# Output weights split in each pass, PSUM-resident convolution sums and column-wise block sums in a hybrid decoder block

## The chip, the cores and the metric

The kernel runs on one core of one Trainium2 chip. Its engines work side by side, each through its own queue in order: TensorE (PE) multiplies, VectorE (DVE), ScalarE (ACT) and GpSimd (POOL) work element by element, SyncE (SP) only issues DMA transfers, as ACT and POOL can too. Operands lie in SBUF; PE writes its products to PSUM, which DVE and ACT read and write. The metric is the device time of one execution in microseconds (us); less is better.

## The reference, cut to what matters

One decoder layer, 16 meta tokens ahead of 1024 tokens, width 1024, two mixing groups of 512 channels, feed-forward width 2816, all fp32:

```python
def mixer(xn, w_in, conv_a_w, conv_b_w, conv_b_bias, ln_b_gain, ln_b_bias, w_out):
    h = jnp.einsum("btd,de->bte", xn, w_in)
    b_gate, c_gate, h_a, glu_val, glu_gate = jnp.split(
        h, [W_A, 2 * W_A, 3 * W_A, 3 * W_A + W_B], axis=-1)
    y_a = b_gate * causal_depthwise_conv(c_gate * h_a, conv_a_w)      # 3 taps
    g = glu_val * jax.nn.sigmoid(glu_gate)
    z = causal_depthwise_conv(g, conv_b_w) + conv_b_bias              # 31 taps
    y_b = jax.nn.silu(layer_norm(z, ln_b_gain, ln_b_bias))
    y = jnp.concatenate([y_a, y_b], axis=-1)
    return jnp.einsum("bte,ed->btd", y, w_out)

h = h + rms_norm(mixer(rms_norm(h, pre_mix_norm), ...), post_mix_norm)
h = h + rms_norm(swiglu(rms_norm(h, pre_ffn_norm), w_gate, w_up, w_down), post_ffn_norm)
```

## The kernel before

Every product is made of three fp32r matmuls (`mm3`, lines 107 to 111): each operand is split into a rounded high part (an ACT copy, names in `h`) and the rest (a subtraction, names in `l`), and high x high, high x low and low x high are summed in PSUM. The order of the instructions on each engine is that of the program text.

**Input projection.** w_in comes in 20 units of 128 output channels; a unit is a letter (g, v: gate and value of the convolution group; c, h, b: the three parts of the other group) and an index 0 to 3. Units (g,0) and (v,0) run while x arrives (lines 178 to 243). Then `UNITS` (line 142) sets the order of the other 18: g1 v1 g2 v2 g3 v3, then c h b for each index. For each unit the loop at line 495 first emits the split of the next unit's weights (`split_unit`: high part on ACT, low on POOL), the load of the one after it, then `after[...]`, which takes the previous unit out of PSUM, then what `LEAD_IN` lists for that step, and last the unit's matmuls on PE. Two units have PSUM at a time, so what takes unit i out must be done when PE begins unit i+2. `AT` puts further work between the matmuls of a step.

**Output weights.** `pre_out` (line 252) loads a 128-row unit of w_out, splits it on ACT and DVE and stores both parts to DRAM (`wo`). Units 0 and 1 are emitted ahead of the end of (v,0), 2 to 5 in step 0, 6 and 7 inside `start_g`, which also spreads the inverse norms over the partitions (`spread_x`, tile pb_x) and makes the first gate.

**Convolution of 31 taps.** Times are kept as even and odd halves of 512 columns (e and o in `gpad`). Per channel block a there are three chains of DVE operations (`taps`, line 338), each sum kept in a PSUM tile: `common` (o with summed taps), then `even` (e - o) and `odd` (a shifted difference). `common` starts from z in SBUF and ends there, and the other two start from z and end there. The two differences are DVE operations on SBUF tiles (lines 352, 353). The first eight terms of `common` for blocks 1 to 3 come from `conv_head` (ACT products, POOL additions into z). `tap(n)` in `LEAD_IN` emits the next n taps. `value` (line 309) writes the gate product into the halves.

**Layer norm.** `ln_sum`, `ln_mean`, `ln_var`, `ln_spread`, `ln_apply` in steps 13 to 16; `sums` adds the four blocks in SBUF.

**Output projection.** Three passes, `group((0,1,2))`, `group((3,4,5))`, `group((6,7))`, over token tiles; a pass takes all 8 units of w_out in the order `up` or `down_`. `next_o` fetches the split units from DRAM on POOL's queue, 18 in all. `leave_psum` and `norms` finish a tile, `turn` transposes it for the next stage.

**Feed-forward.** Both products use a seven-product block scheme. T1 to T4, B11, B21, B22 are the right operands, made from the transposed tiles (`raw`); `a_side` makes the left ones from w_gate and w_up, two products ahead, where `operand` emits the ACT copy and the DVE subtraction of one matrix and then those of the other. `order` lists the products as (pair, n); product s takes its operands from step s - 2. `Pair.leave` takes them out of PSUM.

Of the kernel before, what the change touches and what calls it, by code (L numbers as in the profile page):

```python
# [15 lines left out]
P = 128  # L16
# [41 lines left out]
def hybrid_block(ctx: ExitStack, tc: tile.TileContext, xT, x, w_in, w_out, w_gate, w_up, w_down, par, g_post, g_ffn, g_out, out):  # L58
# [81 lines left out]
    wo = [dram.tile([P, 2, D], F32R, tag=f"wo{k}", name=f"wo{k}") for k in range(KD)]  # L140
# [88 lines left out]
    split_unit(UNITS[0])  # L229
    nc.vector.tensor_tensor(sa[0], sa[0], sa[1], op=ALU.add)  # L230

# [13 lines left out]
    ws_o = {}  # L245

    def load_raw_o(k):
        if k < KD:
            ws_o[k] = yap.tile([P, D], F32, tag="y", name=f"ws_o{k}")
            nc.sync.dma_start(ws_o[k], w_out[k])  # L250

    def pre_out(k):
        load_raw_o(k + 2)
        ws = ws_o.pop(k)
        h, l = (yap.tile([P, D], F32R, tag="y", name=f"{c}_o{k}") for c in ("wh", "wl"))
        nc.scalar.copy(h, ws)
        nc.vector.tensor_tensor(l, ws, h.bitcast(F32), op=ALU.subtract)
        for q, t in enumerate((h, l)):
            nc.sync.dma_start(wo[k][:, q, :].bitcast(F32), t.bitcast(F32))
# [12 lines left out]
    mm_k(pu["v", 0], split_w["v", 0], KD - 1, 0, T3, 3)  # L272
# [36 lines left out]
    def value(a):  # L309
        o4 = new_g(a).rearrange("p r (a n) -> p a n r", a=3)  # L310
        for i in range(3):
            nc.vector.tensor_tensor(o4[:, i], pu["v", a][:, i, :T3].rearrange("p (n r) -> p n r", r=2), three(sg[a])[:, i].rearrange("p (n r) -> p n r", r=2), op=ALU.mult)
# [15 lines left out]
    def conv_head(a):  # L328

        ze, zo = halves_of(a)  # L330
        o = gpad[a][1]
        nc.scalar.activation(zo, o[:, :HALF], AF.Identity, scale=wc(a, 0), bias=pr[:, O_CBB + a : O_CBB + a + 1])
        for i in range(1, HEAD[a]):
            t = ct.tile([P, HALF], F32, tag="ct", name=f"ct{a}{i}")
            nc.scalar.activation(t, o[:, i : i + HALF], AF.Copy, scale=wc(a, i))
            nc.gpsimd.tensor_tensor(zo, zo, t, op=ALU.add)

    def taps(name, src, w, first, n, init, out):
        acc = aux.tile([P, 512], F32, tag="a", name=name)
        for i in range(first, n):  # L340
            nc.vector.scalar_tensor_tensor(out if i == n - 1 else acc, src[:, i : i + HALF], w(i), init if i == first else acc, op0=ALU.mult, op1=ALU.add)  # L341
            yield

    def common(a):
        ze, zo = halves_of(a)
        yield from taps(f"ac{a}", gpad[a][1], lambda i: wc(a, i), HEAD[a], NE, zo, zo)

    def even(a):
        e, o = gpad[a]
        ze, zo = halves_of(a)  # L350
        d = ct.tile([P, (G0 + TT) // 2], F32, tag="d", name=f"d{a}")
        nc.vector.tensor_tensor(d, e, o, op=ALU.subtract)
        nc.vector.tensor_tensor(o[:, :-1], e[:, 1:], o[:, :-1], op=ALU.subtract)
        yield from taps(f"ae{a}", d, lambda i: wb(a, 2 * i), 0, NE, zo, ze)

    def odd(a):
        e, o = gpad[a]
        ze, zo = halves_of(a)
        yield from taps(f"ao{a}", o, lambda i: wb(a, 2 * i + 1), 0, NE - 1, zo, zo)
# [10 lines left out]
    def conv():  # L370
        yield from common(0)
        yield from by_turns(even(0), odd(0))
        yield from by_turns(common(1), common(2))
        yield from by_turns(even(1), odd(1))
        yield from by_turns(even(2), odd(2))
        yield from common(3)
        yield from by_turns(even(3), odd(3))

    conv_taps = conv()
# [28 lines left out]
    def after_b(a):  # L408
        yh[a], yl[a] = (yap.tile([P, SEQ], F32R, tag="y", name=f"y{c}{a}") for c in "hl")
        for q in range(2):  # L410
            s = slice(q * HALF, (q + 1) * HALF)
            nc.vector.tensor_tensor(cv[a][:, s], pu["b", a][:, q, :], cv[a][:, s], op=ALU.mult)  # L412
        nc.scalar.copy(yh[a], cv[a])
        nc.vector.tensor_tensor(yl[a], cv[a], yh[a].bitcast(F32), op=ALU.subtract)
# [8 lines left out]
    def sums(srcs, outs):  # L423
        for q in range(3):
            for hf in range(2):
                nc.vector.tensor_tensor(outs[hf], srcs(hf, 0) if q == 0 else outs[hf], srcs(hf, q + 1), op=ALU.add)

    def ln_sum():
        ln["zs"] = [ct.tile([P, HALF], F32, tag="ct", name=f"zs{hf}") for hf in range(2)]
        sums(lambda hf, a: z[a][:, hs_[hf]], ln["zs"])  # L430

    def ln_mean():
# [8 lines left out]
        sums(lambda hf, a: ln["sq"][hf, a], [ln["sq"][hf, 0] for hf in range(2)])  # L441
# [33 lines left out]
    def start_g():  # L475
# [43 lines left out]
    ps2 = pa.enter_context(tc.tile_pool(name="ps2", bufs=6, space=PSUM, reuse_waits="tile"))  # L519

    for a in range(4):
# [6 lines left out]
        nc.vector.tensor_tensor(ol, z2, oh.bitcast(F32), op=ALU.subtract)  # L528

# [69 lines left out]
    def operand(src, name, place=None):  # L599
# [6 lines left out]
        sub(t[:, 1, :], src, t[:, 0, :].bitcast(F32))  # L606
# [11 lines left out]
    class Pair:  # L618
# [19 lines left out]
        def a_side(self, n, m, place=None):  # L638
# [21 lines left out]
            return operand(s, f"{n}_{self.j}{m}", place)  # L660
# [74 lines left out]
    wu = {}  # L735

    def load_o(k):
        wu[k] = [wp.tile([P, D], F32R, tag=t, name=f"{t}_o{k}") for t in ("wh", "wl")]
        for q in range(2):
            nc.gpsimd.dma_start(wu[k][q], wo[k][:, q, :])  # L740

    todo_o = list(range(KD)) + list(range(KD - 4, -1, -1)) + list(range(3, KD))

    def next_o():
        if todo_o:
            load_o(todo_o.pop(0))

    def group(grp, ks, at):
# [8 lines left out]
        for s, k in enumerate(ks[:-2]):  # L757
# [3 lines left out]
            if s or grp[0] == 0:  # L761
                next_o()
# [16 lines left out]
    for q, t in ((0, 0), (1, 1), (0, 1), (1, 0)):  # L779
        raw[q, t] = blocks(big(f"raw{q}{t}", F32))  # L780
# [6 lines left out]
    s1, left = group((3, 4, 5), down_, {4: turns(0, 1), 5: turns(2)})  # L787
# [49 lines left out]
    s1, left = group((6, 7), up, {6: early})  # L837
# [21 lines left out]
    def t2():  # L859
        X[6] = pair("T2", (rp, rp))  # L860
        copy_hi(X[6], T2r)
        split_lo(X[6], T2r)
# [351 lines left out]
```

## Time and profile before

| | us |
|---|---|
| median of 3 runs (lowest, highest) | 1059.92 (1058.63, 1061.58) |
| the profiled execution | 1059.18 |
| its span, first to last instruction | 1057.2 |
| input projection, (v,0) ends to (b,3) ends | 35 to 279 |
| output projection and entry of the products | 279 to 387 |
| gate and up products | 387 to 828 |
| down products and the end | 828 to 1057 |

The profile records one execution. Its page gives busy time by engine, 40 slices of the span, DMA queues and the costliest groups of instructions; other views of the trace give the same by stretch of time, the waits of each engine with what ended them, and the instructions in order. L341 is line 341 of the kernel, `ae<-d,pr,z` a write of tile ae from d, pr and z, and `x4` a count.

### The profile page before, as it was taken

The page shows a single profiled execution, that of the slowest core. Times are in us where ns is not written, and L with a number is a line of the kernel's source. Part 1 is how long each engine was busy: PE and PEld are TensorE (multiplying, and loading weights), DVE is VectorE, ACT ScalarE, POOL GpSimd, SP SyncE. Part 2 cuts the span into 40 slices and gives each one's busy share as a digit, 9 for nine tenths or more (in the row PEclk, how much of TensorE's full clock was granted, in tenths as well). Part 3 has the DMA queues.
Part 4 walks back from the last instruction along what each step waited for, and adds up shares of the span by engine and source line. Part 5 has one row for each costly group of instructions (what it writes and reads, how often), then busy time and mean ns, then how long its engine had stood idle before and what let it go on. Part 6 is the DMA issues. An engine that isn't in the chain of part 4 may idle for free.

```text
span 1057.2 us, 12732 instructions
## 1 busy us (share of the span) xinstructions
PE 986.2 (93%) x4643; PEld 839.9 (79%) x4643; DVE 773.9 (73%) x1087; ACT 378.4 (36%) x616; POOL 296.3 (28%) x267
## 2 busy tenths in 40 slices
PE   9599998879999797998999999999999899999994
PEld 8499998769787675876888888888888788888773
DVE  6689999997414558789888888888878343446667
ACT  7433331233413254333443433434334233322331
POOL 0247774443112100026134223313413522212110
PEclk9799998989999999999999999999999999999998
DMA  7851111001759552034634443353324989867765
GB/s 304 301 216 41 41 42 60 20 20 61 254 163 316 183 184 74 1 122 177 219 130 149 160 170 148 130 209 117 142 100 169 384 309 376 270 183 204 268 215 209
DMA packets 64909, 180.80 MB, mean 171 GB/s; under 512 B 6864, under 2 KB 7248, under 8 KB 64848
## 3 DMA queue, kind: packets, MB, share of 16 engines
q1 hardware_dynamic: 43344, 109.40, 28.2%
q0 software_dynamic: 16272, 59.25, 17.4%
q10 hardware_dynamic: 5232, 11.35, 3.0%
q8 instruction: 36, 0.59, 0.2%
q14 instruction: 25, 0.20, 0.1%
HBM read 122.83 MB, written 57.15 MB: 170 GB/s over the span
## 4 chain that ended last, share of the span: by engine, by line
PE 60%; DVE 26%; DMA 5%; ACT 4%; issue 4%; POOL 1%; SPq 0%; DVEq 0%; ACTq 0%; POOLq 0%
PE x L109 6%; PE x L111 6%; PE x L110 6%; PE y L109 5%; PE y L110 5%; PE y L111 5%; DVE ao L341 4%; DVE ae L341 4%; PE qx L110 3%; PE qx L109 3%; PE qx L111 3%; DVE ac L341 3%; PE qy L110 2%; PE qy L111 2%; PE qy L109 2%
## 5 line engine op out<-in xcount | busy, mean ns | idle before, releaser
L592 DVE TENSOR_TENSOR op<-u,op 128x512 fp32r<-128x512 f32 x154 | 142.9, 955 | 61.6 <-ACT op L605 61.6
L605 ACT CAST op<-u 128x512 fp32r<-128x512 f32 x154 | 90.7, 618 | 163.6 <-DVE u L592 153.6
L592 DVE TENSOR_TENSOR db<-wb,db 128x512 fp32r<-128x512 f32 x77 | 53.7, 701 | 93.2 <-ACT db L1015 92.9
L1015 ACT CAST db<-wb 128x512 fp32r<-128x512 f32 x77 | 47.0, 621 | 117.4 <-PE qx L111 55.2
L595 POOL TENSOR_TENSOR C<-C,C 128x512 f32<-128x512 f32 x11 | 15.4, 1400 | 246.8 <-ACT C L705 246.8
L109 PE MATMUL qx<-db,a 128*128 128x512 f32 x176 | 68.7, 390 | 3.2 <-DMA a<-gdA 3.2
L110 PE MATMUL qx<-db,a 128*128 128x512 f32 x176 | 68.7, 390 | 0.4 <-DVE db L592 0.3
L111 PE MATMUL qx<-db,a 128*128 128x512 f32 x176 | 68.5, 389 | 0.0
L595 POOL TENSOR_TENSOR U<-U,U 128x512 f32<-128x512 f32 x22 | 31.2, 1419 | 92.1 <-ACT U L705 83.4
L109 PE MATMUL qy<-db,a 128*128 128x512 f32 x132 | 51.5, 390 | 0.5 <-ACT db L1015 0.5
L110 PE MATMUL qy<-db,a 128*128 128x512 f32 x132 | 51.5, 390 | 0.3 <-DVE db L592 0.3
L111 PE MATMUL qy<-db,a 128*128 128x512 f32 x132 | 51.4, 389 | 0.0
L991 POOL DMA_DIRECT2D a<-gdS x44 | 23.3, 531 | 92.2 <-PE qy L111 47.2
L589 DVE TENSOR_TENSOR U<-y,U 128x512 f32<-128x512 f32 x66 | 42.7, 681 | 7.8 <-PE y L111 7.8
L341 DVE SCALAR_TENSOR_TENSOR ae<-d,pr,ae 128x512 f32<-128x512 f32 x56 | 41.8, 747 | 0.0
L109 PEld LDWEIGHTS qx<-db,a 128*128 128x128 f32 x176 | 33.0, 188 | 10.8 <-ACT U L705 3.6
L109 PE MATMUL y<-T2h,op 128*128 128x512 f32 x88 | 35.5, 403 | 5.6 <-DVE G L595 4.4
L592 DVE TENSOR_TENSOR u<-u,u 128x512 f32<-128x512 f32 x44 | 39.9, 907 | 0.8
L109 PE MATMUL x<-B21h,op 128*128 128x512 f32 x88 | 35.0, 398 | 5.3 <-ACT U L677 5.3
L109 PE MATMUL p_h<-xh,wh_h 128*128 128x342 f32 x96 | 32.8, 341 | 7.3 <-DVE cv L412 7.3
L110 PEld LDWEIGHTS qx<-db,a 128*128 128x128 f32 x176 | 33.0, 188 | 7.9 <-DVE db L592 1.2
L341 DVE SCALAR_TENSOR_TENSOR ao<-g,pr,ao 128x512 f32<-128x512 f32 x52 | 38.8, 747 | 0.0
(290 smaller groups left out, 3015.1 us busy)
## 6 DMA issues: line engine op xcount, KB each, us to landing
a<-gdS POOLq DMA_DIRECT2D x44, 512.0 KB, 4.7
a<-gdA POOLq DMA_DIRECT2D x33, 512.0 KB, 5.8
u<-w_gate_u SPq DMA_DIRECT2D x22, 512.0 KB, 5.4
u<-w_up_u SPq DMA_DIRECT2D x22, 512.0 KB, 5.9
gdS<-HI SPq DMA_DIRECT2D x44, 256.0 KB, 2.3
wh_o<-wo POOLq DMA_DIRECT2D x18, 512.0 KB, 5.8
wl_o<-wo POOLq DMA_DIRECT2D x18, 512.0 KB, 7.2
gdA<-HI SPq DMA_DIRECT2D x33, 256.0 KB, 2.0
```

Of the source, the lines that this page charges most:

```text
L109: nc.tensor.matmul(o, lh, rh, start=start, stop=False, skip_group_check=again)
L110: nc.tensor.matmul(o, lh, rl, start=False, stop=False, skip_group_check=again)
L111: nc.tensor.matmul(o, ll, rh, start=False, stop=stop, skip_group_check=again)
L341: nc.vector.scalar_tensor_tensor(out if i == n - 1 else acc, src[:, i : i + HALF], w(i), init if i == first else acc, op0=ALU.mult, op1=AL ...
L589: (eng or nc.vector).tensor_tensor(o, a, b, op=ALU.add)
L592: (eng or nc.vector).tensor_tensor(o, a, b, op=ALU.subtract)
L595: (eng or nc.vector).tensor_tensor(o, a, b, op=ALU.mult)
L605: nc.scalar.copy(t[:, 0, :], src)
L991: nc.gpsimd.dma_start(loads[n, j], gd[an][j])
L1015: nc.scalar.copy(t[:, 0, :], b)
```

## The change

It has these parts:

- `wo` in DRAM, `pre_out` and `next_o` go. `load_o(k)` loads a raw unit of w_out on SP into the weight ring, `split_o(k)` splits it, in each pass again. Units 3 and 4 are held in SBUF over the three passes; the second pass takes the units in the order 5 6 7 3 4 0 1 2 and so begins with three that are still there, the third begins with 0 1 2. 14 loads and splits in all. The first loads of w_gate and w_up move from ahead of pass one into pass three.
- At the entry, the low parts of the first two units of the loop move to DVE, `ss_x` moves behind the last matmuls of (v,0), the two copies out of PSUM move ahead of the norms' small operations, and `start_g` one k later.
- The chains of the convolution begin and end in PSUM: `both` is filled by ACT, the common chain adds to it, and the two other chains start from it. The differences move to POOL, ahead of the chains, and change e in place of o. The tap counts per step are new; three taps of it are emitted inside `after_b`, between the ACT copy and the subtraction.
- `add_up` keeps the middle sums of the layer norm in PSUM.
- `value` and `start_g` write the halves column by column instead of pair by pair.
- In the products, `a_side` emits both matrices' sums, then both ACT copies, then both subtractions; T2 is made in two halves, earlier; T4 gets its tiles earlier.

```diff
-    def split_unit(u):
+    def split_unit(u, eng=None):
...
+    def load_o(k):
+        raw_w["o", k] = wp.tile([P, D], F32, tag="ws", name=f"ws_o{k}")
+        nc.sync.dma_start(raw_w["o", k], w_out[k])
+
+    def split_o(k, eng=None):
+        if k in (3, 4):
+            wu[k] = [held[k - 3][:, q, :] for q in range(2)]
+        else:
+            wu[k] = [wp.tile([P, D], F32R, tag=t, name=f"{t}_o{k}") for t in ("wh", "wl")]
+        nc.scalar.copy(wu[k][0], raw_w["o", k])
+        (eng or nc.vector).tensor_tensor(wu[k][1], raw_w["o", k], wu[k][0].bitcast(F32), op=ALU.subtract)
...
-    split_unit(UNITS[0])
     nc.vector.tensor_tensor(sa[0], sa[0], sa[1], op=ALU.add)
+    split_unit(UNITS[0], nc.vector)
...
-    for k in range(2):
-        load_raw_o(k)
-    for k in range(2):
-        pre_out(k)
...
     mm_k(pu["v", 0], split_w["v", 0], KD - 2, 0, T3, 3)
+    mm_k(pu["v", 0], split_w["v", 0], KD - 1, 0, T3, 3)
...
-    mm_k(pu["v", 0], split_w["v", 0], KD - 1, 0, T3, 3)
...
-        o4 = new_g(a).rearrange("p r (a n) -> p a n r", a=3)
+        o3 = new_g(a)
+        n = T3 // 2
         for i in range(3):
-            nc.vector.tensor_tensor(o4[:, i], pu["v", a][:, i, :T3].rearrange("p (n r) -> p n r", r=2), three(sg[a])[:, i].rearrange("p (n r) -> p n r", r=2), op=ALU.mult)
+            nc.vector.tensor_tensor(o3[:, :, i * n : (i + 1) * n], pu["v", a][:, i, :T3].rearrange("p (n r) -> p r n", r=2), three(sg[a])[:, i].rearrange("p (n r) -> p r n", r=2), op=ALU.mult)
...
+    def differences(a):
+
+        e, o = gpad[a]
+        dd[a] = ct.tile([P, (G0 + TT) // 2], F32, tag="d", name=f"d{a}")
+        nc.gpsimd.tensor_tensor(dd[a], e, o, op=ALU.subtract)
+        nc.gpsimd.tensor_tensor(e[:, 1:], e[:, 1:], o[:, :-1], op=ALU.subtract)
...
+    def conv(a):
+        e, o = gpad[a]
+        ze, zo = halves_of(a)
+        both = aux.tile([P, 512], F32, tag="a", name=f"ac{a}")
+        if HEAD[a] > 1:
+            nc.scalar.copy(both, zo)
+        else:
+            nc.scalar.activation(both, o[:, :HALF], AF.Identity, scale=wc(a, 0), bias=pr[:, O_CBB + a : O_CBB + a + 1])
+        yield from taps(o, lambda i: wc(a, i), HEAD[a], NE, both, both, both)
+        ae = aux.tile([P, 512], F32, tag="a", name=f"ae{a}")
+        yield from by_turns(taps(dd[a], lambda i: wb(a, 2 * i), 0, NE, both, ae, ze), taps(e[:, 1:], lambda i: wb(a, 2 * i + 1), 0, NE - 1, both, both, zo))
...
         nc.scalar.copy(yh[a], cv[a])
+        if a < 3:
+            tap(3)
+            rest_y(a)
+
+    def rest_y(a):
         nc.vector.tensor_tensor(yl[a], cv[a], yh[a].bitcast(F32), op=ALU.subtract)
...
-    def sums(srcs, outs):
+    def add_up(srcs, mids, outs):
         for q in range(3):
             for hf in range(2):
-                nc.vector.tensor_tensor(outs[hf], srcs(hf, 0) if q == 0 else outs[hf], srcs(hf, q + 1), op=ALU.add)
+                nc.vector.tensor_tensor(outs[hf] if q == 2 else mids[hf], srcs(hf, 0) if q == 0 else mids[hf], srcs(hf, q + 1), op=ALU.add)
...
+    taps_ = {1: 13, 3: 14, 5: 14, 7: 16, 9: 10, 10: 16, 11: 14}
+    LEAD_IN = {i: (lambda n=n: tap(n)) for i, n in taps_.items()}
+    LEAD_IN.update({2: begin(1, 14), 4: begin(2, 14), 6: some(lambda: conv_head(3), lambda: tap(14)), 8: some(lambda: differences(3), lambda: tap(14))})
+    LEAD_IN.update({12: lambda: tap(40), 13: ln_sum, 16: ln_apply, 17: gains})
+    AT = {(0, 2): start_g, (14, 1): ln_mean, (15, 3): ln_var, (15, 7): ln_spread}
...
-            split_unit(UNITS[i + 1])
+            split_unit(UNITS[i + 1], nc.vector if i == 0 else None)
+        else:
+            split_o(0, nc.gpsimd)
...
+    split_o(1, nc.gpsimd)
+    load_o(2)
     after_b(3)
-    scale_gains()
+    rest_y(3)
...
+        if a == 0:
+            split_o(2)
+            load_o(3)
+    scale_gains()
...
-    pairs[0].load(0)
-    pairs[1].load(0, (0,))
-    s1, left = group((0, 1, 2), up, {})
+    s1, left = group((0, 1, 2), up, {0: ahead(3, 5), 1: ahead(4, 6), 2: ahead(5, 7), 3: ahead(6, 0), 4: ahead(7, 1), 6: ahead(None, 2)})
...
-    s1, left = group((3, 4, 5), down_, {4: turns(0, 1), 5: turns(2)})
+    s1, left = group((3, 4, 5), middle, {1: ahead(0, 5), 2: ahead(1, 6), 3: ahead(2, 7), 4: turns(0, 1), 5: turns(2)})
...
-    s1, left = group((6, 7), up, {6: early})
+    s1, left = group((6, 7), up, {1: ahead(5), 2: lambda: [split_o(6), pairs[0].load(0)], 3: pairs_load, 6: early})
...
-        made[s] = [pairs[j].a_side(n, m, places[m] if places else None) for m in range(2)]
+        src = sums.pop(s, None) or [pairs[j].a_side(n, m) for m in range(2)]
+        t = [operand_hi(src[m], f"{n}_{j}{m}", places[m] if places else None) for m in range(2)]
+        for m in range(2):
+            sub(t[m][:, 1, :], src[m], t[m][:, 0, :].bitcast(F32))
+        made[s] = t
...
+    X[6] = pair("T2", (rp, rp))
     a_side(3)
-    for i in range(2):
-        t2_sum(i)
...
+    for f in (t2_sum, t2_hi, t2_lo):
+        for i in range(2):
+            f(i)
...
             turns(6, 7)()
+            sums[4] = [pairs[0].a_side(6, m) for m in range(2)]
...
         if s == 2:
+            for f in (t1_sum, t2_sum, t2_hi):
+                for i in range(2, 4):
+                    f(i)
+            a_side(4)
             for i in range(2, 4):
-                t1_sum(i)
-                t2_sum(i)
+                t2_lo(i)
```

`ahead(k, n)` splits unit k and then loads unit n; `begin(a, n)` emits `differences(a)`, n taps and `conv_head(a)`; `pairs_load` splits unit 7 and loads the first half of w_gate for pair 1.

More of the change, by code (lines that the diff above doesn't have):

```diff
@@ L271, in hybrid_block, with three @@
         nc.tensor.matmul(ss[: c.stop - c.start, i : i + 1], sa[0][:, c], ones[:, :1], start=True, stop=True)
-    mm_k(pu["v", 0], split_w["v", 0], KD - 1, 0, T3, 3)
+    def three(t):
+        return t.rearrange("p (a b) -> p a b", a=3)
+    sg = {0: row(tp, "t", "sg0", TT)}
+    vs = row(tp, "t", "vs0", TT)
+    nc.scalar.copy(three(sg[0]), pu["g", 0][:, :, :T3])
+    nc.scalar.copy(three(vs), pu["v", 0][:, :, :T3])
     nc.vector.tensor_copy(sx[:, :NT], ss[:, :NT])
@@ L290, in spread_x @@
         nc.gpsimd.tensor_tensor(r2, rB, rB, op=ALU.mult)
-    gpad, sg = {}, {}
-    def three(t):
-        return t.rearrange("p (a b) -> p a b", a=3)
+    gpad = {}
     def gate(a):
@@ L328, in conv_head, with taps @@
     def conv_head(a):
[L330 to L339, printed above, removed]
+        if HEAD[a] > 1:
+            ze, zo = halves_of(a)
+            o = gpad[a][1]
+            nc.scalar.activation(zo, o[:, :HALF], AF.Identity, scale=wc(a, 0), bias=pr[:, O_CBB + a : O_CBB + a + 1])
+            for i in range(1, HEAD[a]):
+                t = ct.tile([P, HALF], F32, tag="ct", name=f"ct{a}{i}")
+                nc.scalar.activation(t, o[:, i : i + HALF], AF.Copy, scale=wc(a, i))
+                nc.gpsimd.tensor_tensor(zo, zo, t, op=ALU.add)
+    dd = {}
+    def differences(a):
[3 more added lines that the diff above has]
+        nc.gpsimd.tensor_tensor(e[:, 1:], e[:, 1:], o[:, :-1], op=ALU.subtract)
+    def taps(src, w, first, n, init, acc, out):
         for i in range(first, n):
@@ L342, in taps @@
             yield
[L344 to L359, printed above, removed]
     def by_turns(*gens):
@@ L368, in by_turns, with all_taps @@
                     yield
[L370 to L379, printed above, removed]
+    def conv(a):
+        e, o = gpad[a]
+        ze, zo = halves_of(a)
+        both = aux.tile([P, 512], F32, tag="a", name=f"ac{a}")
+        if HEAD[a] > 1:
+            nc.scalar.copy(both, zo)
[4 more added lines that the diff above has]
+        yield from by_turns(taps(dd[a], lambda i: wb(a, 2 * i), 0, NE, both, ae, ze), taps(e[:, 1:], lambda i: wb(a, 2 * i + 1), 0, NE - 1, both, both, zo))
+    def all_taps():
+        for a in range(4):
+            yield from conv(a)
+    conv_taps = all_taps()
     def tap(n):
@@ L440, in ln_mean @@
             nc.scalar.activation(ln["sq"][hf, a], z[a][:, hs_[hf]], AF.Square)
-        sums(lambda hf, a: ln["sq"][hf, a], [ln["sq"][hf, 0] for hf in range(2)])
+        ln["sp"] = [aux.tile([P, 512], F32, tag="a", name=f"qp{hf}") for hf in range(2)]
+        add_up(lambda hf, a: ln["sq"][hf, a], ln["sp"], [ln["sq"][hf, 0] for hf in range(2)])
     def ln_var():
@@ L597, in hybrid_block, with operand_hi @@
     n_ops = [0]
-    def operand(src, name, place=None):
+    def operand_hi(src, name, place=None):
         pool, tag = place or (wp, ("wh", "wl")[n_ops[0] % 2])
@@ L636, in load, with a_side @@
                 self.u[m, i] = t
-        def a_side(self, n, m, place=None):
+        def a_side(self, n, m):
             a11, a12 = self.u[m, 0][:, :512], self.u[m, 0][:, 512:]
@@ L659, in a_side @@
                 s = a22
-            return operand(s, f"{n}_{self.j}{m}", place)
+            return s
         def product(self, n, ops):
@@ L733, in sums @@
                 del v[k]
[L735 to L746, printed above, removed]
     def group(grp, ks, at):
@@ L768, in group, with ahead, f @@
         return s1, {i: leave_psum(i, pm[i], s1, q) for q, i in enumerate(grp)}
-    up, down_ = list(range(KD)), list(range(KD - 1, -1, -1))
-    for q in range(3):
-        next_o()
+    def ahead(k=None, n=None):
+        def f():
+            if k is not None:
+                split_o(k)
+            if n is not None:
+                load_o(n)
+        return f
+    up, middle = list(range(KD)), [5, 6, 7, 3, 4, 0, 1, 2]
+    load_o(4)
     hs = {i: residual_x(i) for i in (0, 1, 2)}
     pairs = {j: Pair(j) for j in range(3)}
-    pairs[0].load(0)
-    pairs[1].load(0, (0,))
-    s1, left = group((0, 1, 2), up, {})
+    s1, left = group((0, 1, 2), up, {0: ahead(3, 5), 1: ahead(4, 6), 2: ahead(5, 7), 3: ahead(6, 0), 4: ahead(7, 1), 6: ahead(None, 2)})
     B11 = [blocks(big(f"B11{j}", pool=bp)) for j in "hl"]
-    for q, t in ((0, 0), (1, 1), (0, 1), (1, 0)):
-        raw[q, t] = blocks(big(f"raw{q}{t}", F32))
+    for q in range(2):
+        raw[q, 0] = blocks(big(f"raw{q}0", F32))
     hn = norms((0, 1, 2), left, s1, hs)
@@ L800, in t2_sum, with t2_hi, t2_lo @@
         sub(T2r[:, :, c], r22[:, :, c], r11[:, :, c])
+    def t2_hi(i):
+        c = slice(i * P, (i + 1) * P)
+        nc.scalar.copy(X[6][0][:, :, c], T2r[:, :, c])
+    def t2_lo(i):
+        c = slice(i * P, (i + 1) * P)
+        sub(X[6][1][:, :, c], T2r[:, :, c], X[6][0][:, :, c].bitcast(F32))
     def split_lo(o, src):
@@ L816, in hybrid_block @@
     order += [(j, n) for j in range(2, NP) for n in (1, 6, 2, 5, 7, 3, 4)]
-    made = {}
+    made, sums = {}, {}
     LEAD = 2
@@ L825, in a_side, with pairs_load @@
             pairs[j + 1] = Pair(j + 1)
-        made[s] = [pairs[j].a_side(n, m, places[m] if places else None) for m in range(2)]
+        src = sums.pop(s, None) or [pairs[j].a_side(n, m) for m in range(2)]
[3 more added lines that the diff above has]
+        made[s] = t
+    def pairs_load():
+        split_o(7)
+        pairs[1].load(0, (0,))
     def early():
+        for q in range(2):
+            raw[q, 1] = blocks(big(f"raw{q}1", F32))
         turns(3, 4, 5)()
         pairs[1].load(0, (1,))
-        t1_sum(0)
-        t1_sum(1)
+        for i in range(2):
+            t1_sum(i)
         a_side(0)
@@ L854, in hybrid_block @@
     st = ctx.enter_context(tc.tile_pool(name="st", bufs=11, reuse_waits="tile"))
+    X[6] = pair("T2", (rp, rp))
     a_side(3)
-    for i in range(2):
-        t2_sum(i)
[L859 to L862, printed above, removed]
+    for f in (t2_sum, t2_hi, t2_lo):
+        for i in range(2):
+            f(i)
     def t1():
@@ L871, in t3 @@
         X[7] = pair("T3", (rp, None))
+        T4.append(blocks(big("T4l")))
         copy_hi(X[7], r12)
@@ L875, in b22 @@
     def b22():
+        T4.append(blocks(big("T4h")))
         X[3] = pair("B22", (rp, None))
@@ L880, in t4 @@
     def t4():
+        l, h = T4
+        X[4] = h, l
         halves(sub, r21, r21, T2r)
-        X[4] = pair("T4", (None, None))
         copy_hi(X[4], r21)
```

53 lines of the change are left out of this document (19 added, 34 removed).

## The prediction

> **What bounds the kernel now.** I read the page's engine table first, then a table by stages, then what TensorE (PE) waited for.
>
> ```profile
> span 1057.2 us, 12732 instructions
> PE 986.2 (93%) x4643; PEld 839.9 (79%) x4643; DVE 773.9 (73%) x1087; ACT 378.4 (36%) x616; POOL 296.3 (28%) x267
> ```
>
> PE is busy 93% of the span, so no other engine can give more than PE's lost time. The stages show where that lies. Columns: stretch, its length, busy time of PE, weight load, DVE, ACT, POOL, with instructions, then granted clock, DMA share, GB/s.
>
> ```profile
> 28.00:62.30 34.30, 22.01 (x119) 21.05 (x118) 22.84 (x26) 13.78 (x16) 10.25 (x6) 0.75 0.90 343
> 62.33:119.66 57.33, 57.33 (x361) 57.33 (x361) 53.61 (x66) 19.87 (x25) 39.31 (x24) 1.00 0.17 62
> 164.90:242.40 77.50, 64.04 (x317) 57.49 (x318) 74.49 (x93) 20.23 (x24) 33.22 (x14) 0.89 0.09 29
> 279.10:387.00 107.90, 97.13 (x434) 77.71 (x433) 46.05 (x93) 34.34 (x68) 16.93 (x32) 0.97 0.69 236
> 387.00:433.00 46.00, 38.27 (x163) 30.38 (x162) 37.15 (x69) 20.66 (x36) 0.00 (x0) 0.93 0.20 69
> 433.00:510.00 77.00, 70.63 (x302) 57.33 (x301) 65.19 (x79) 29.92 (x48) 22.50 (x14) 0.98 0.32 121
> 510.00:828.00 318.00, 317.99 (x1403) 263.05 (x1402) 264.50 (x337) 126.39 (x227) 92.50 (x64) 1.00 0.44 160
> 831.30:860.00 28.70, 28.70 (x127) 23.76 (x128) 9.15 (x14) 7.49 (x12) 10.59 (x14) 1.00 0.95 320
> ```
>
> From 510 to 828 us PE has no hole, and the diff leaves it nothing to gain there. Two prices come from full-clock rows: 57.33/360 = 0.159 us for a matmul of 342 or 348 columns, 318/1403 = 0.227 us for one of 512. What PE lost before 510 us, with each wait's total, times and longest:
>
> ```profile
> PE pb_x L286 <- ACT rB L289: 10.6, 1, 10.6
> PE p_h L109 <- DVE cv L412: 7.3, 2, 3.9
> PE pm L435 <- DVE zs L426: 6.2, 1, 6.2
> PE x L109 <- ACT U L677: 5.3, 2, 4.1
> PE y L109 <- DVE G L595: 4.4, 1, 4.4
> PE po L110 <- DMA wl_o<-wo: 3.9, 4, 1.8
> PE po L109 <- DMA wh_o<-wo: 3.5, 1, 3.5
> PE qx L109 <- DMA a<-gdA: 3.2, 1, 3.2
> PE pt L573 <- ACT raw L575: 2.9, 4, 1.2
> ```
>
> Each stretch with such waits also has a clock below 1, so a hole costs more than its length. I compare each stretch with its matmuls at full clock.
>
> **Entry, 28.0 to 62.3.** Here PE issues the last 18 matmuls of (v,0), 72 of (g,1) and some small ones.
>
> ```profile
> 31.26 2.08 PE L271 MATMUL ss_x<-ones,sa 128*128 128x1 f32 x18 [1.66 <-DVE sa L230]
> ...
> 49.31 1.11 PE L286 MATMUL pb_x<-ident,s_x 128*128 128x128 f32 x4 [10.63 <-ACT rB L289]
> ```
>
> ```profile
> 35.96 0.17 DVE L131 SCALAR_TENSOR_TENSOR s_x<-t_x,s_x 128x9 f32<-128x9 f32 x1
> ```
>
> ```profile
> 48.13 1.04 ACT L256 CAST wh_o<-ws_o 128x1024 fp32r<-128x1024 f32 x1 [3.31 <-DMA ws_o<-w_out_u]
> ```
>
> The inverse norms are ready at 36.1, but ACT stands in its queue behind the first splits of the output weights, which wait for loads and stores, and evacuates pb_x only after 49. The change takes all eight `pre_out` off ACT, DVE and SP here; nothing of them returns before unit (b,3). The addition for which ss_x waited ran beside a POOL split; that split and the next move to DVE behind it, ahead of PE's need, and ss_x behind the last of p_v, at 1.2 us each by the median of the same subtraction here (minimum, median, maximum).
>
> ```profile
> L257 DVE TENSOR_TENSOR wl_o<-ws_o,wh_o x8: 1210/1226/2527, 31.1 to 56.8; 128x1024 fp32r<-128x1024 f32 x8
> ```
>
> Late next is PE itself. Unit (v,1), with which the second stretch of the table begins, can start at 28.0 + 18 x 0.159 + 2.1 + 1.1 + 72 x 0.159 = 45.5, plus 0.8 that I allow for the other transposes and one small ACT copy between them: 46.3 against 62.3. **Gain 16.0.**
>
> **Convolution, 62 to 242.** PE falls behind only where DVE is late: p_h waits for L412, pm for L426. DVE's groups between 57 and 246 us (count, busy, mean ns):
>
> ```profile
> L341 DVE SCALAR_TENSOR_TENSOR ac<-g,wsum,ac 128x512 f32<-128x512 f32 x31 | 22.4, 751 | 0.6
> L426 DVE TENSOR_TENSOR sq<-sq,sq 128x512 f32<-128x512 f32 x6 | 10.0, 1723 | 0.0
> L341 DVE SCALAR_TENSOR_TENSOR ae<-d,pr,z 128x512 f32<-128x512 f32 x4 | 9.3, 2337 | 0.0
> L341 DVE SCALAR_TENSOR_TENSOR ao<-g,pr,z 128x512 f32<-128x512 f32 x4 | 9.3, 2335 | 0.0
> L353 DVE TENSOR_TENSOR g<-g 128x526 f32<-128x526 f32 x4 | 8.9, 2221 | 0.2
> L352 DVE TENSOR_TENSOR d<-g 128x527 f32<-128x527 f32 x4 | 6.9, 1718 | 0.0
> L341 DVE SCALAR_TENSOR_TENSOR ac<-g,wsum,z 128x512 f32<-128x512 f32 x4 | 6.7, 1683 | 3.0 <-ACT z L332 1.8 <-POOL z L336 1.2
> L312 DVE TENSOR_TENSOR g<-p_v,sg 128x348 f32<-128x348 f32 x9 | 6.1, 786 | 0.0
> ```
>
> A tap with its sum in PSUM takes 0.75 us, one whose start comes from z in SBUF 1.7 to 2.3, while POOL works. With starts in PSUM the twelve slow first taps fall from 25.3 to 9.0 (-16.3), the eight differences (15.8) leave DVE, and the square sums lose perhaps 4. Added: two common chains no longer run in turns, so 16 taps wait for each other, for which I allow 0 to 2 us, and each chain's start waits for one ACT copy behind the last tap but one; the low parts of y only move. L312 by columns lies between 0.79, unchanged, and nothing; it hides either way. So DVE loses some 32 us where it cost PE 19.9 (below), and it starts 16 earlier, as PE does: about 12 us of cover, against which stand two-input instructions that POOL may still hold (low parts of y, three before the mean, up to 2 each). All three waits go.
>
> The differences go to POOL, where the trace has none of them; two rows bound each:
>
> ```profile
> L336 POOL TENSOR_TENSOR z<-z,ct 128x512 f32<-128x512 f32 x21 | 29.9, 1425 | 22.5 <-ACT ct L335 21.0
> L405 POOL TENSOR_TENSOR cv<-cv,u 128x1024 f32<-128x1024 f32 x6 | 15.2, 2528 | 38.2 <-ACT u L404 38.0
> ```
>
> From below 1.4, the first row, to 2.5, the second, of twice the width; I take 1.4, as its width is nearest: 8 x 1.4 = 11 us in a queue that stands idle 22.5 us before that group alone. Behind them queue the heads' additions and the w_in splits, for which PE waits one unit (72 x 0.159 = 11.4) later; a pair of differences at 2.5 makes POOL 2.2 later, still covered.
>
> PE's need from 164.9 on: 216 x 0.159 + 96 x 0.227 + 1.5, an allowance for the mean's two fp32 products, = 57.6 of 77.5. **Gain 19.9.**
>
> **Output projection, 279 to 387.** PE needs 384 x 0.227 + 48 transposes at 2.08/18 = 0.116 = 92.7 of 107.9. Two 512 KB transfers per unit and step go; one raw load and a split per unit come, 14 in all.
>
> ```profile
> ws_o<-w_out_u SPq DMA_DIRECT2D x8, 512.0 KB, 8.5
> ```
>
> A raw load took 8.5 us in the entry's full queues; here it is issued two or three steps of 18 x 0.227 = 4.1 us ahead. So the po waits on DMA (7.4) go. A split costs ACT 1.04 and DVE 1.2 (rows above), but it queues on DVE behind the norms. Pass two ended just before this ACT row, and DVE's norms ran until 366.5:
>
> ```profile
> 350.96 0.60 ACT L537 ACTIVATE sq<-po 128x512 f32<-128x512 f32 x1 [1.35 <-PE po L111]
> ```
>
> ```profile
> 362.86 3.68 DVE L565 SCALAR_TENSOR_TENSOR hn<-h,s_pf,gB_ffn 128x1024 f32<-128x1024 f32 x3
> ```
>
> That is 15.7 us into pass three; the low part of unit 5 follows at 16.9, and PE wants it after five steps of 2.7, at 13.8: a **new hole of 3.1**. Likewise in pass two the splits of units 0 to 2 stand ahead of the first transposed block, 0.7 late. A clock of 0.97 over 107.9 is 6.5 us at half speed, 3.2 lost, after holes of 3.5 and 1.8; for one of 3.1 I take half, 1.6. Left over the need: 0.7 (L412) + 2.9 at pt + 0.7 + 3.1 + 1.6 = 9.0 of 15.2. **Gain 6.**
>
> The qx wait of 3.2 left the clock at 1.00 in the stretch from 831. By the Trainium skill, TensorE: Matmul & The Clock Gate, section Why this matters for your kernels, PE should not idle over about 3 us between bursts, or one window puts it back to half speed. By that row the sum would be 1.6 better, by the rule it stays; no row here shows a hole of just 3.1.
>
> **Products, 387 to 510.** PE needs 144 x 0.227 + 16 x 0.116 = 34.5 of 46.0, then 302 x 0.227 = 68.6 of 77.0.
>
> ```profile
> 421.49 0.68 DVE L595 TENSOR_TENSOR G<-x,G 128x512 f32<-128x512 f32 x1
> ```
>
> G of pair 1 releases PE at 422.2; it stands in DVE's queue behind T2's low halves and operand sums, each with a turn to ACT. T2 earlier and both copies ahead of both subtractions shorten that queue by some 3 us; but T2's first copies now precede the turned blocks on ACT (+1.4 before product 3), and w_up's second half lands late as before. I take 4.6 of 11.5 here, and 3.4 of 8.4 after it, where U waits 4.1 for ACT, from the shorter turns. Bounds: 0 and 19.9; I stay nearer the low end, as DVE was busy 37 of 46. **Gain 8.**
>
> **Sum.** 16.0 + 19.9 + 6 + 8 = 49.9; 1057.2 - 49.9 = 1007.3, plus 2.0 outside the span (1059.2 in the profiled execution) = 1009.3, plus 0.7, as the median 1059.9 lies that much above: **1010**.
>
> **Rivals.** (a) Entry and convolution gain, passes and products turn their waits into DVE's: 14 less, 1024. For it: DVE's queue in both. (b) The remaining holes go too, 9.0 + 6.9 + 5.0: 990 to 1004. Against it: the norms' chain, which nothing shortens. (c) The PSUM starts do not free DVE, because POOL, now with the differences, holds what DVE still has with two SBUF inputs, and the heads come late for the chains: the 19.9 stays, 1030. Against it: only some 20 such instructions are left there. The Trainium skill's SBUF — State Buffer, Who interferes with whom, has the second to issue blocked for the whole instruction; the 2.3 us first taps agree. (d) **Slower**: the passes starve. If a unit's load, ACT copy and subtraction run in series (8.5 + 1.0 + 1.2 = 10.7 against a step of 4.1, or 2.7 in pass three), 11 x 6.6 + 3 x 8.0 = 97 are lost against 44 won: 1113. It decides once a cycle exceeds three steps, 12.3, because three raw buffers turn, so once a load takes over 10.1; against it, the passes move 7 MB of weights in place of 19 (36 transfers of 512 KB).
>
> **Chances.** Forecast (1004 to 1016) 0.55, (a) 0.18, (b) 0.15, (c) 0.07, (d) 0.03, no net change 0.02. The range 998 to 1026 takes in (a) and half of (b). A difference of 0.3% is what a measurement here can tell from none: faster 0.95, same 0.02, slower 0.03.
>
> **What would show it.** Right: unit (v,1) starts near 46 us, no PE wait on L412 or the z sums, no po wait on DMA but one on DVE of 2 to 3.5 us in pass three, clock 1.00 from 55 to 240. Wrong: pb_x still over 2 us late; first taps over 1 us; DVE busy to the end of unit (c,3); po waiting on ACT or raw loads.

## The result, and the profile after

The changed kernel takes 1004.63 us (median of 4 runs, 1003.76 to 1006.32) against 1060.24 before (4 runs): a ratio of 0.9478, 95% interval 0.9460 to 0.9496. In us below, a difference of ratios is multiplied by 1060. The profiled execution took 1006.32 with a span of 1004.5, 52.7 less than before. The page, span and engines first, then the loads of the output weights (count, size, median us from issue to landing):

```profile
span 1004.5 us, 12668 instructions
PE 971.9 (97%) x4643; PEld 831.7 (83%) x4643; DVE 739.9 (74%) x1087; ACT 388.1 (39%) x627; POOL 280.0 (28%) x239
...
ws_o<-w_out_u SPq DMA_DIRECT2D x14, 512.0 KB, 4.8
```

A raw load lands after 4.8 us, far from the 10.1 at which rival (d) would decide.

The table by stages (stretch, length, busy PE, weight load, DVE, ACT, POOL, clock, DMA share, GB/s), cut where the same work begins and ends as in the stages before:

```profile
28.00:45.87 17.87, 17.87 (x121) 17.59 (x120) 10.10 (x21) 7.58 (x9) 5.01 (x4) 1.00 0.18 60
45.87:103.20 57.33, 57.33 (x362) 57.33 (x361) 53.97 (x78) 20.30 (x26) 43.60 (x30) 1.00 0.14 47
103.20:148.40 45.20, 45.20 (x267) 43.10 (x266) 43.09 (x62) 14.44 (x18) 29.19 (x18) 1.00 0.14 47
148.40:206.10 57.70, 57.70 (x317) 52.59 (x316) 45.69 (x63) 19.70 (x24) 32.72 (x14) 1.00 0.14 46
206.10:242.54 36.44, 36.44 (x218) 34.29 (x216) 20.26 (x32) 14.23 (x13) 9.19 (x4) 1.00 0.23 79
242.54:343.55 101.01, 95.50 (x433) 78.21 (x432) 59.62 (x105) 45.95 (x80) 0.00 (x0) 0.98 0.40 144
343.55:778.50 434.95, 425.22 (x1865) 350.49 (x1864) 363.69 (x487) 180.03 (x315) 114.08 (x78) 0.99 0.41 151
```

PE has no hole from 28 to 242.5, and the clock is 1.00 there. Against the same stages before, the entry ends 16.4 us earlier (45.87 for 62.3), the convolution is 20.1 shorter (196.7 for 216.8), the passes 6.8 (101.0 for 107.8, 279.1 to 386.94) and the products up to the first down product 9.3 (434.95 for 444.3, 386.94 to 831.23); what follows takes 226.0 in both. What PE still waits for (total, times, longest):

```profile
PE pt L590 <- ACT raw L592: 4.1, 4, 1.6
PE x L109 <- ACT U L693: 3.9, 2, 2.7
PE po L110 <- DVE wl_o L169: 2.3, 1, 2.3
PE qx L109 <- DMA a<-gdA: 2.3, 1, 2.3
PE y L109 <- DVE G L612: 2.0, 1, 2.0
```

pb_x, p_h and pm are gone from the list, and po waits no more for a transfer. For the convolution, these rows show the first taps of the even chains and the additions of two squares on DVE, then the differences on POOL (count, busy, mean ns, idle before):

```profile
L344 DVE SCALAR_TENSOR_TENSOR ae<-d,pr,ac 128x512 f32<-128x512 f32 x4 | 3.0, 756 | 0.2
L424 DVE TENSOR_TENSOR qp<-sq,sq 128x512 f32<-128x512 f32 x2 | 4.8, 2456 | 0.0
L339 POOL TENSOR_TENSOR d<-g 128x527 f32<-128x527 f32 x4 | 5.3, 1334 | 15.1 <-DVE g L310 7.3 <-DVE z L344 5.3 <-DVE g L481 2.5
L340 POOL TENSOR_TENSOR g<-g 128x526 f32<-128x526 f32 x4 | 4.5, 1118 | 0.3
```

### The profile page after: what moved, and what is told of

The parts are those of the page before. It is cut to its first block, busy times and chain, and to the rows that moved or that the text cites. A ratio compares the mean times of both kernels' runs of the same rounds, so it can differ in the third digit from the quotient of the medians.

```text
span 1004.5 us, 12668 instructions
## 1 busy us (share of the span) xinstructions
PE 971.9 (97%) x4643; PEld 831.7 (83%) x4643; DVE 739.9 (74%) x1087; ACT 388.1 (39%) x627; POOL 280.0 (28%) x239
## 4 chain that ended last, share of the span: by engine, by line
PE 81%; DVE 12%; issue 3%; ACT 2%; DMA 2%; SPq 0%; DVEq 0%; ACTq 0%; POOL 0%; POOLq 0%
PE x L111 6%; PE x L109 6%; PE x L110 6%; PE y L109 5%; PE y L111 5%; PE y L110 5%; PE qx L110 3%; PE qx L109 3%; PE qx L111 3%; PE qy L110 3%; PE qy L111 3%; PE qy L109 3%; PE po L110 2%; PE po L111 2%; PE po L109 2%
## 5 line engine op out<-in xcount | busy, mean ns | idle before, releaser
L609 DVE TENSOR_TENSOR op<-u,op 128x512 fp32r<-128x512 f32 x154 | 145.8, 980 | 24.4 <-ACT op L622 23.4
L612 POOL TENSOR_TENSOR C<-C,C 128x512 f32<-128x512 f32 x11 | 17.6, 1597 | 332.6 <-ACT C L721 183.0
L344 DVE SCALAR_TENSOR_TENSOR ac<-g,pr,ac 128x512 f32<-128x512 f32 x56 | 41.9, 748 | 0.0
L109 PEld LDWEIGHTS qx<-db,a 128*128 128x128 f32 x176 | 33.0, 188 | 9.8 <-issue 2.7
L110 PEld LDWEIGHTS qx<-db,a 128*128 128x128 f32 x176 | 33.0, 188 | 7.9 <-DVE db L609 1.1
L111 PEld LDWEIGHTS qx<-db,a 128*128 128x128 f32 x176 | 33.1, 188 | 6.8
```

The source lines that it names most:

```text
L109: nc.tensor.matmul(o, lh, rh, start=start, stop=False, skip_group_check=again)
L110: nc.tensor.matmul(o, lh, rl, start=False, stop=False, skip_group_check=again)
L111: nc.tensor.matmul(o, ll, rh, start=False, stop=stop, skip_group_check=again)
L609: (eng or nc.vector).tensor_tensor(o, a, b, op=ALU.subtract)
L612: (eng or nc.vector).tensor_tensor(o, a, b, op=ALU.mult)
```

## The experiments

Each starts from the changed kernel, and "+" is time against it. The interval of each ratio reaches 1.4 to 3 us to either side, so a difference below some 3 us is not told from none.

**Entry: which part of the old work cost the time?** Three kernels put back all of it, the transfers alone, and the engine work alone.

```diff
+    def pre_out(k):
+        load_raw_o(k + 2)
+        ws = ws_o.pop(k)
+        nc.scalar.copy(h, ws)
+        nc.vector.tensor_tensor(l, ws, h.bitcast(F32), op=ALU.subtract)
+        for q, t in enumerate((h, l)):
+            nc.sync.dma_start(wo[k][:, q, :].bitcast(F32), t.bitcast(F32))
```

> The changed kernel with all eight splits of the output weights put back into the entry, at their old places (raw load, ACT copy, DVE subtraction, two stores to DRAM); their results are not read, and the passes still split each unit themselves, so the work stands there in addition. Theory, the removed work held ACT's queue: PE waits for the inverse norms at pb_x again (before: 10.6 us, 16.4 us lost in the entry), the time rises by 12 to 17 us. Rival, the gain came from what was reordered in the entry (sum of squares, two splits on DVE): the time rises by under 4 us.

> The changed kernel with only the transfers of the old entry put back: eight raw loads and sixteen stores of 512 KB on SP's queue, no ACT copy and no DVE subtraction; nothing reads them. Theory, ACT's queue: no engine that PE waits for stands behind these transfers, so 0 to 2 us. Rival, the traffic itself slows the loads of the input weights: 5 us or more, with PE waiting for wh_g or wh_v.

> The changed kernel with only the engine work of the old entry put back: eight ACT copies (1.04 us) and eight DVE subtractions (1.2 us) on data that already lies in SBUF, no transfer; their results are not read. If the copies wait mainly for their loads, six copies and some subtractions ahead of pb_x cost at most their own time behind the inverse norms: 2 to 7 us. If the work itself was the price: 10 us or more. If neither: under 2.

Measured: all of it 0.9612 (0.9588 to 0.9637), +14.2; transfers alone 0.9499 (0.9473 to 0.9525), +2.2; engine work alone 0.9481 (0.9465 to 0.9496), +0.3. ACT's instructions in the first kernel, from 38 us on (idle before in brackets):

```profile
38.63 1.04 ACT L270 CAST wh_p<-ws_p 128x1024 fp32r<-128x1024 f32 x1 [4.64 <-DMA wo<-wh_p]
42.53 1.04 ACT L270 CAST wh_p<-ws_p 128x1024 fp32r<-128x1024 f32 x1 [2.86 <-DMA ws_p<-w_out_u]
46.44 1.04 ACT L270 CAST wh_p<-ws_p 128x1024 fp32r<-128x1024 f32 x1 [2.87 <-DMA ws_p<-w_out_u]
47.38 0.67 ACT L311 ACTIVATE rB<-pb_x 128x16 f32<-128x16 f32 x2
```

Three copies wait 10.4 us for a store or a load, and the copy of pb_x queues behind them: PE's wait at pb_x is 11.0 again. With the engine work alone it is 0.3, and the copy of pb_x starts at 36.84 in place of 47.38: less than the 2 to 7 us expected of copies that stand ahead of it. The transfers and the engine work are each nearly free; their coupling in ACT's queue is the price. The theory holds. The 2 us between 14.2 and the 16.4 of the entry are within the interval; what was reordered in the entry was not undone.

**Convolution: starts, differences, or order?** First each of the two named edits undone, then both.

```diff
-        nc.gpsimd.tensor_tensor(dd[a], e, o, op=ALU.subtract)
+        nc.vector.tensor_tensor(dd[a], e, o, op=ALU.subtract)
...
-        yield from taps(o, lambda i: wc(a, i), HEAD[a], NE, both, both, both)
+        yield from taps(o, lambda i: wc(a, i), HEAD[a], NE, zo, ac, zo)
```

> The changed kernel with the eight differences back on DVE, each pair behind its common chain; the chains still begin and end in PSUM. Theory, cover: the table by stages has DVE idle for 17.5 us between 45.9 and 206.1, and the differences add 8 x 2 = 16: 0 to 5 us, with PE waiting a little at p_h or pm. Rival, the differences are the part that set PE's waits: 10 to 20 us. Second rival, POOL was late with them: the time falls by 1 or more.

> The changed kernel with the chains of the convolution beginning and ending in z in SBUF as before; the differences stay on POOL. Theory, cover: the twelve first taps are held by POOL again (0.76 to some 2 us each, 15 us in all), DVE has 17.5 us idle between 45.9 and 206.1: 0 to 4 us. Rival, the starts alone made the gain of the convolution: 10 us or more, with PE waiting at p_h and pm.

> The changed kernel with both undone: differences on DVE and chains that begin and end in SBUF. Each alone fits into DVE's 17.5 us of idle time; both together add 16 to 20 for the first taps and the differences' 9.5 (measured with PSUM starts) to 16 (as before): 26 to 36. By the cover theory PE loses what exceeds 17.5, and what DVE can no longer catch up: 8 to 18 us, with waits at p_h and pm as before. Rival, the gain came from elsewhere (earlier start of DVE, order of the low parts of y): under 4 us.

Measured: differences on DVE 0.9479 (0.9463 to 0.9495), +0.1; chains through SBUF 0.9486 (0.9473 to 0.9499), +0.8; both 0.9550 (0.9536 to 0.9565), +7.6, just below the 8 to 18 expected and far from 20.1; PE then waits 1.5 and 1.3 us for DVE at p_c, not at p_h or pm. So I undid every edit of the convolution, and then all but the values by columns and the sums in PSUM:

```diff
-        for a in range(4):
-            yield from conv(a)
+        yield from common(0)
+        yield from by_turns(even(0), odd(0))
+        yield from by_turns(common(1), common(2))
...
```

> The changed kernel with every edit of the convolution undone: differences on DVE, chains through SBUF, chains 1 and 2 in turns, the old counts of taps, the low parts of y straight behind their copies, values pair by pair. Entry, passes and products stay changed. Theory, the old order is what let POOL hold the first taps (2.3 us each before; 1.0 to 1.8 with only the two undone, which gave back 7.9 us): 16 to 22 us slower, PE waiting at p_h and pm. Rival, the rest of the gain came from the entry, which handed DVE over with less in its queue: 6 to 10 us slower, as with the two.

> The kernel with every edit of the convolution undone (22.8 us slower than the changed one), but with the values by columns and the sums over the four channels through PSUM, as in the changed kernel; so what stays undone are the differences on DVE, the chains through SBUF, the order and counts of taps and the place of y's low parts. Theory, the order decides how long POOL holds the first taps and differences (41 us of DVE in the old order, 26 in the new one): the first taps stay at 1.7 to 2.3 us, and the kernel stays 15 us or more slower than the changed one. Rival, the values by columns and the sums (about 8 us of DVE) shift DVE out of POOL's way: 7 to 11 us slower, as with the two edits undone in the new order.

Measured: everything undone 0.9693 (0.9667 to 0.9719), +22.8; with columns and PSUM sums kept 0.9666 (0.9638 to 0.9695), +19.9, and PE waits at p_h (8.3) and pm (5.5) as before. DVE's groups, first in the kernel with both edits undone in the new order:

```profile
L344 DVE SCALAR_TENSOR_TENSOR ac<-g,wsum,z 128x512 f32<-128x512 f32 x4 | 7.3, 1814 | 1.8 <-ACT z L361 1.8
L340 DVE TENSOR_TENSOR g<-g 128x526 f32<-128x526 f32 x4 | 5.9, 1472 | 0.1
L339 DVE TENSOR_TENSOR d<-g 128x527 f32<-128x527 f32 x4 | 4.9, 1223 | 0.0
L344 DVE SCALAR_TENSOR_TENSOR ae<-d,pr,z 128x512 f32<-128x512 f32 x4 | 4.0, 1011 | 0.0
L344 DVE SCALAR_TENSOR_TENSOR ao<-g,pr,z 128x512 f32<-128x512 f32 x4 | 4.0, 1010 | 0.0
```

and the same operations in the old order:

```profile
L335 DVE SCALAR_TENSOR_TENSOR ae<-d,pr,z 128x512 f32<-128x512 f32 x4 | 9.4, 2338 | 0.0
L335 DVE SCALAR_TENSOR_TENSOR ao<-g,pr,z 128x512 f32<-128x512 f32 x4 | 9.3, 2332 | 0.0
L347 DVE TENSOR_TENSOR g<-g 128x526 f32<-128x526 f32 x4 | 8.9, 2220 | 0.2
L346 DVE TENSOR_TENSOR d<-g 128x527 f32<-128x527 f32 x4 | 6.8, 1699 | 0.0
L335 DVE SCALAR_TENSOR_TENSOR ac<-g,wsum,z 128x512 f32<-128x512 f32 x4 | 6.7, 1685 | 3.0 <-ACT z L326 1.8 <-POOL z L330 1.2
```

The same twenty instructions take 26.1 us in one order and 41.1 in the other. In the old order the pair of chains for block 3 begins while POOL works on cv; DVE and POOL, in order of time:

```profile
178.20 2.79 DVE L347 TENSOR_TENSOR g<-g 128x526 f32<-128x526 f32 x1
180.91 2.90 DVE L335 SCALAR_TENSOR_TENSOR ae<-d,pr,z 128x512 f32<-128x512 f32 x1
183.72 2.87 DVE L335 SCALAR_TENSOR_TENSOR ao<-g,pr,z 128x512 f32<-128x512 f32 x1
186.51 0.74 DVE L335 SCALAR_TENSOR_TENSOR ae<-d,pr,ae 128x512 f32<-128x512 f32 x1
```

```profile
175.19 5.23 POOL L399 TENSOR_TENSOR cv<-cv,u 128x1024 f32<-128x1024 f32 x2 [15.04 <-ACT u L398]
180.50 2.75 POOL L400 TENSOR_TENSOR cv<-cv,rB 128x1024 f32<-128x1024 f32 x1
183.21 2.82 POOL L154 TENSOR_TENSOR wl_h<-ws_h,wh_h 128x1024 fp32r<-128x1024 f32 x1
```

Each of the three DVE instructions that read two SBUF tiles ends 0.6 us after a POOL instruction; the next tap, with its sum in PSUM, takes 0.74. The order theory holds: undoing starts and differences costs 7.6, undoing the order with them 19.9, so 12.3 more. Order here means the order of the chains, the tap counts, the place of the heads and of y's low parts, and the half that the second difference overwrites; these were undone together and not told apart. What the old order costs with PSUM starts was not tried, as the two PSUM tiles of the chains are both taken while two common chains run in turns.

**Passes: low parts on POOL.** The hole of 2.3 in pass three waits for DVE's queue, while POOL stands idle. The edit of pass three is shown; the units of pass two are changed in the same way.

```diff
-    s1, left = group((6, 7), up, {1: ahead(5), 2: lambda: [split_o(6), pairs[0].load(0)], 3: pairs_load, 6: early})
+    s1, left = group((6, 7), up, {1: ahead(5, None, nc.gpsimd), 2: lambda: [split_o(6, nc.gpsimd), pairs[0].load(0)], 3: pairs_load, 6: early})
```

> The changed kernel with the low parts of the units split in passes two and three (0, 1, 2 and 5, 6, 7) made on POOL, which stands idle there, in place of DVE. Theory, the hole of 2.3 us in pass three is DVE's queue: it goes, and the half clock of 3.4 us behind it (1.7 lost) too: 3 to 4 us faster. Rival, POOL's subtractions hold DVE's norms, which read two operands in SBUF, by up to 2.5 us each, and the transposed blocks come late: 0 to 4 us slower.

Measured 0.9565 (0.9548 to 0.9581), +9.2, where the theory had 3 to 4 faster and the rival at most 4 slower: the hole goes, and PE waits 6.9 for hn instead. DVE between the squares and hn behind pass two, then POOL:

```profile
288.24 0.16 DVE L130 TENSOR_TENSOR t_pf<-t_pf,v_pf 128x3 f32<-128x3 f32 x1
288.44 2.39 DVE L131 SCALAR_TENSOR_TENSOR s_pf<-t_pf,s_pf 128x3 f32<-128x3 f32 x1
290.86 2.32 DVE L129 TENSOR_TENSOR t_pf<-s_pf 128x3 f32<-128x3 f32 x1
293.22 2.31 DVE L130 TENSOR_TENSOR t_pf<-t_pf,v_pf 128x3 f32<-128x3 f32 x1
```

```profile
288.42 7.09 POOL L169 TENSOR_TENSOR wl_o<-ws_o,wh_o 128x1024 fp32r<-128x1024 f32 x3 [46.22 <-DVE t_pf L130]
```

The rival's mechanism holds, at another place than it said: the three POOL subtractions hold not the wide scalings but three steps of the inverse norm, three numbers wide, for a whole subtraction each.

**Products.** T2's place alone, then all edits of the products' order.

```diff
-    for f in (t2_sum, t2_hi, t2_lo):
-        for i in range(2):
-            f(i)
+    for i in range(2):
+        t2_sum(i)
...
-        l, h = T4
-        X[4] = h, l
+        X[4] = pair("T4", (None, None))
```

> The changed kernel with T2 made as before: its sums in turns with T1's, its copies and low halves behind product 3; copies ahead of subtractions stay. Theory, T2's early parts shortened DVE's queue before G: the wait for G returns from 2.0 to about 4.4 with a half clock behind it, 3 to 5 us slower. Rival, the order of copies and subtractions made the gain of the products: 0 to 1 us.

> The changed kernel with every edit of the products' order undone: T2 late, T4's buffers taken at its own step, each operand's copy and subtraction in turns. Theory, these edits shortened DVE's queue and ACT's turns (T2's place alone gave 0.8 us): 5 to 9 us slower, with the waits for T4, U and G back. Rival, the gain of the products came with the passes that hand over earlier: 0 to 2 us.

Measured: T2 late 0.9486 (0.9472 to 0.9500), +0.8, the rival's figure (the wait for G is 3.0 in place of 2.0, one at pt 1.4 shorter); all undone 0.9574 (0.9551 to 0.9598), +10.2, with these waits:

```profile
PE y L109 <- DVE G L612: 4.5, 1, 4.5
PE qx L109 <- DMA a<-gdA: 3.4, 1, 3.4
PE x L109 <- ACT U L693: 3.3, 2, 2.2
...
PE x L109 <- ACT op L622: 1.5, 1, 1.5
```

The stage of the products, 341.69 to 786.02, takes 444.3 us again, as before, for 434.95; the half clock of pass three is gone here (1.9 less ahead of the stage), and one behind the hole at qx has come (2.9 more behind it). So the gain is the products' own, and T2 is not enough for it; T4's tiles and the order of copies and subtractions were not tried one by one.

**A version against the remaining holes.** Four edits at the places where PE still waits, two of them shown.

```diff
+            results.pop(1)()
             turns(6, 7)()
...
-        if s in (14, 15):
+        if s == 14:
```

> A further version of the changed kernel, four edits at its remaining holes: in pass three the low parts of units 5 to 7 go ahead of the last scaling of the rows (hole of 2.3 and its half clock, 1.7); at product 2 the copies of U go ahead of the last transposed blocks, and T2's first copies behind them (1.2 of 1.2, 1.4 of 1.6, half clock 1.7); at product 15 the copies of U go ahead of the halves that wait for stores (2.7 and 1.7); in pass two one transposed block per step (1.2). If no other queue is late behind them: 10 to 14 us faster. Rival, DVE's queue takes over at each of these places: 2 to 5 us faster.

Measured 0.9467 (0.9444 to 0.9489), 1.2 us faster, which cannot be told from none and is below what the rival expected. The edit at product 15 does its part (stretch 440 to 470: PE 27.54 busy at clock 0.94 in the changed kernel, here full):

```profile
440.00:470.00 30.00, 30.00 (x131) 24.04 (x130) 29.13 (x37) 13.92 (x26) 9.87 (x7) 1.00 0.69 251
770.00:800.00 30.00, 26.80 (x107) 21.59 (x106) 8.31 (x12) 7.59 (x12) 13.87 (x19) 0.89 0.84 294
```

```profile
PE y L109 <- ACT op L628: 3.3, 1, 3.3
PE qx L109 <- DMA a<-gdA: 3.2, 1, 3.2
PE x L109 <- ACT op L628: 2.0, 1, 2.0
...
PE y L110 <- DVE T2l L615: 1.7, 1, 1.7
```

But PE then meets operands and T2 that are late on ACT and DVE, and at qx a transfer, in the profiled execution with a half clock behind it. No version better than the changed kernel is shown.

## Why the prediction was right, point by point

The total was 1010 against 1004.6, at the low edge of the forecast's 1004 to 1016 and next to rival (b)'s 990 to 1004. All four terms have the right size: 16.0, 19.9, 6 and 8 against 16.4, 20.1, 6.8 and 9.3. Each is a little low, so no errors cancelled; they make 2.8 of the 5.4 us missed. The rest is that the profiled execution of the changed kernel was its slowest, where the sum put it below the median.

- **Entry.** Shown as argued: ACT's queue behind loads and stores; nothing late comes in its place.
- **Convolution.** The waits go, as forecast. DVE's busy time in the stage falls by 31.4 us (194.4 to 163.0) against 32, the differences take 1.1 to 1.3 us on POOL against 1.4, and the sums of squares lose 2.6 (10.0 to 7.4) against 4. But the step that named the causes fell short. It gave the order of the chains a price of 0 to 2 us; the runs show that the order is itself a cure, at least where the chains start in SBUF: first taps fall from 25.4 to 15.3 us by order alone, where the step put all 16.3 down to the starts, and the differences from 15.7 to 10.8. The cover taken as 12 us was larger too: DVE is idle 17.5 of the 160.2 us between 45.87 and 206.1, so undoing either named edit costs nothing that the interval shows (0.1 and 0.8). Rival (c) had the mechanism right, POOL holding DVE, and the outcome wrong.
- **Passes.** The new hole came where it was put, in pass three behind the norms, 2.3 against 3.1, and a half clock behind it (1.7 against 1.6). That the half clock came is in part luck: the last section has the same hole without one. The gain is read from stages and waits; no run undid it.
- **Products.** The size was right; 0.9 of the 9.3 is the shorter wait at qx (3.2 to 2.3), which the step did not count. But T2's place, to which the step gave part of the gain, is worth 0.8 alone, no more than the interval allows for nothing; only all edits undone take the stage back to 444.3. Rival (b), the remaining holes, was tried: they move.

## What to carry to other kernels

Splitting an engine's cost into its work and its waits pays: here 14 us came from copies that waited for transfers ahead of a copy that PE needed, while both alone were nearly free. Where idle time covers each of several edits, undoing them one by one shows nothing; undo them together, and count the order of the instructions as an edit. Before work moves to an idle POOL, look for DVE instructions with two SBUF inputs beside it, small ones too, on a chain that PE waits for.

## What the hardware showed that was not expected

A POOL instruction holds a DVE instruction of 128x3 (0.16 us) for 2.3 to 2.4 us, as it holds one of 128x512 for 2.9, and again for the next: 7.0 us for three, beside three subtractions that take 7.1. The Trainium skill, SBUF — State Buffer, Who interferes with whom, says of the ports that DVE and GpSimd share that whoever issues first has them for the whole instruction and the other is blocked; these rows agree.

The same hole of 2.30 us in pass three halved the clock in the changed kernel and not in the one with chains through SBUF. In the clock records of all fourteen traces the granted clock changes only on a grid: the time between any two changes is a multiple of 3.41 us. These rows are neighbouring windows of that grid (busy PE third, clock third from the end), two of the changed kernel, then two of the other:

```profile
327.45:330.86 3.41, 1.46 (x6) 1.24 (x7) 3.41 (x4) 0.00 (x0) 0.00 (x0) 1.00 0.83 287
330.86:334.27 3.41, 3.41 (x12) 2.77 (x11) 0.75 (x1) 0.14 (x1) 0.00 (x0) 0.50 0.89 303
```

```profile
324.52:327.93 3.41, 2.19 (x10) 1.50 (x8) 3.41 (x4) 0.05 (x1) 0.00 (x0) 1.00 0.38 118
327.93:331.34 3.41, 2.33 (x10) 1.95 (x11) 3.30 (x3) 0.00 (x0) 0.00 (x0) 1.00 0.77 282
```

In the changed kernel 1.95 us of the hole fall into one window, and the next window runs at half clock. In the other kernel the hole is split, 1.22 and 1.08, and the clock stays at 1.00 (the window behind them has it too). The wait of 3.2 at qx before was split likewise, 1.70 and 1.53, and left the clock whole. In the fourteen traces, from 10 us on, PE idles 1.86 us or more in 49 windows at full clock, and a half clock follows each; with 1.85 or less none follows, but for two windows near 31 us with under 0.3 us of idle time, whose cause stays open.

So a hole's length alone does not decide, but how much of it falls into one window. The Trainium skill, TensorE: Matmul & The Clock Gate, Why this matters for your kernels, sets the limit at about 3 us between bursts; here 2.3 was enough once, and the measurement decides. The grid lies at another place against the program from trace to trace, and a window at half clock costs 1.7 us, so times that differ by 1 to 2 us between these kernels can come from this.
